# The output projection of a hybrid layer's mixed branches: eight block products, and seven by Strassen's scheme

## The chip, the cores and the metric

The kernel runs on one core of one Trainium2 chip, in one launch. The metric is the device time of that launch in microseconds, the median of several runs. The five engines that the profile shows are PE (TensorE, matmuls and transposes; PEld is its weight load), DVE (VectorE), ACT (ScalarE), POOL (GpSimd) and SP (SyncE, which here only issues transfers). Each engine works through its own instructions in order and waits at semaphores for the others.

## The reference

One layer over 512 tokens of width 1024, all in float32. Two mixers (an S5 state space model and NSA attention) run from the same normed input, a sigmoid gate weighs each, and their sum goes through the output projection `w_out`. A convolutional FFN, a gated embedding and a last norm follow.

```
n1 = rmsnorm(x, g_mix);  z = n1 @ w_in
y_ssm = s5_mixer(...);   y_nsa = nsa_mixer(...)
merge = sigmoid(z[:, OFF_MERGE:])                       # 2 x 1024 gates
mixed = merge[:, :1024] * (y_ssm @ w_br_ssm) + merge[:, 1024:] * (y_nsa @ w_br_nsa)
h = x + mixed @ w_out                                   # 512x1024 @ 1024x1024: the change is here
h = h + conv_ffn(rmsnorm(h, g_ffn), w_up, conv_w, conv_b, w_down)
h = h + sigmoid(rmsnorm(h, g_ple) @ w_ple_gate) * (p @ w_ple_proj)
return rmsnorm(h, g_final)
```

## The kernel before

A float32 product is made of three matmuls. Each operand is split into a high part (a rounded copy, made by ACT, line 75) and a low part (the difference of the operand and its high part, made by DVE or POOL, line 54); `split` writes both. `mm3` then issues high times high, high times low and low times high (lines 82, 83, 84), 128 rows by 512 columns each, into one PSUM bank.

A weight of 128 x 1024 values (two to eight blocks of 128 rows) takes four steps. SP loads it into a raw buffer `wr`, of which there are three in rotation; ACT writes `wh` and DVE or POOL writes `wl`, two of each in rotation; PE reads them. A raw buffer is free when its low part has been written, and `wh` and `wl` are free when PE has read them. `wraw` is the load alone, `wload` the load and the split.

The stages around the change, in the order in which PE meets them:

- The attention of 16 units (head and branch), with the matmuls of gates and of the SSM branch product put between its steps as filler (`fillers`, `gate`, `ssm_branch`). The last five gates run on PE with nothing between: 24 matmuls each (`pj`, eight k steps by three), high and low parts of the weights from ACT and POOL, and a tanh on ACT into `t2` (line 944).
- `oS`, the split of the attention's output `oT`, in four pieces on ACT and DVE.
- The NSA branch product: four weights of 256 columns, two tiles `br` of 12 matmuls each. DVE puts each tile onto `t2` (two instructions, line 63), and `t2` holds the mixed branches, transposed: eight blocks of 128 of the 1024 values by 512 tokens.
- The output projection. `t2` is split into `mTh` and `mTl`. `w_out` is loaded in eight pieces of 128 x 1024 and split into `w0h`, `w0l`, `w1h`, `w1l` (the two halves of the columns). Eight tiles `wo`, of four token blocks by two column halves, take 24 matmuls each and DVE adds half of each onto `hres`, which holds x.
- After two token blocks are done, their norm: squares with a sum on ACT (`sq`), a chain of small DVE instructions (`rv`, `ry`, `rt`), the scaled rows `xg`, transposes on PE (`nt`), and from them `n2h` (ACT) and `n2l` (DVE), from which the FFN's up projection reads (`ua`, `ub`). The FFN starts with the first 256 tokens.

The code gives the engines' work in one order, and a scheduler puts each engine's instructions in their final one; `issue_after` holds instructions back behind another. Buffers are shared through tags: a tile of the same tag waits until the earlier one has been read for the last time.

Of the kernel before, what the change touches and what calls it, by code (L numbers as in the profile page):

```python
# [44 lines left out]
def hybrid_kernel(ctx: ExitStack, tc: tile.TileContext, A, out):  # L45
# [1135 lines left out]
    sB.close()  # L1181

    pm_ = sY.enter_context(pool("mix", 1, "right"))
    mTh = pm_.tile([P, KD, T], F32R, name="mTh")
    w0h = pm_.tile([P, KD, 512], F32R, name="w0h")
    hres = slot(cp, "h16", [P, NQ, D], F32, "hres")
    oS = slot(pa, "kv", [P, 2, 4, T], F32R, "oS")
    with tc.issue_after(attended[0]), tc.issue_after(attended[1]):
        for i in range(4):
            split(oS[:, 0, i], oS[:, 1, i], oT[:, i])  # L1190
# [23 lines left out]
    w0l = [slot(py, "y8", [P, 4, 512], F32R, "w0l0"), slot(pa, "v8", [P, 4, 512], F32R, "w0l1")]

    w1h, w1l = (slot(p, t, [P, KD, 512], F32R, n) for p, t, n in ((po, "y16", "w1h"), (pa, "kv", "w1l")))
    for hf in range(2):
        for c in range(4):
            ks, k4 = slice(2 * c, 2 * c + 2), slice(2 * (c % 2), 2 * (c % 2) + 2)
            keep = (w1h[:, ks], w1l[:, ks]) if hf else (w0h[:, ks], w0l[c // 2][:, k4])  # L1220
            wload("w_out", D, 2 * c * P, hf * 512, 2, 512, (G, V)[hf], keep=keep)
# [5 lines left out]
    for qp in range(2):
        for hf, qt in ((0, 0), (0, 1), (1, 0), (1, 1)) if qp == 0 else ((0, 2), (1, 2), (0, 3), (1, 3)):
            cs = slice(hf * 512, hf * 512 + 512)
            qs_ = slice(qt * P, (qt + 1) * P)  # L1230
            ps = bank(either(), "wo")
            for k in range(KD):
                mm3(ps, mTh[:, k, qs_], mTl(k)[:, qs_], (w0h, w1h)[hf][:, k],
                    w1l[:, k] if hf else w0l[k // 4][:, k % 4], k == 0, k == KD - 1)
            stt(hres[:, qt, cs], ps, 0.5, hres[:, qt, cs], MUL, ADD)
# [537 lines left out]
```

## Time and profile before

| | |
|---|---|
| median of 3 runs | 799.89 us (799.82 to 800.62) |
| the profiled execution | 799.49 us, of which the span of the instructions is 797.8 us |
| granted TensorE clock | 0.998 |
| PE busy | 788.5 us, 99% of the span |
| the last five gates | 294.8 to 322.0 us |
| NSA branch product | 322.0 to 343.7 us |
| output projection | 344.1 to 390.1 us |

The profile shows one execution on the core. Busy time counts an instruction from its start to its end; matmuls overlap, so the step from one start to the next is what a matmul costs, not its length. A row of a timeline has the start, the length, the engine, the line, the operation, what it writes and reads, and in square brackets how long the engine had been idle before and who ended that.

### The profile page before, as it was taken

The page shows a single profiled execution, that of the slowest core. Times are in us where ns is not written, and L with a number is a line of the kernel's source. Part 1 is how long each engine was busy: PE and PEld are TensorE (multiplying, and loading weights), DVE is VectorE, ACT ScalarE, POOL GpSimd, SP SyncE. Part 2 cuts the span into 40 slices and gives each one's busy share as a digit, 9 for nine tenths or more (in the row PEclk, how much of TensorE's full clock was granted, in tenths as well). Part 3 has the DMA queues.
Part 4 walks back from the last instruction along what each step waited for, and adds up shares of the span by engine and source line. Part 5 has one row for each costly group of instructions (what it writes and reads, how often), then busy time and mean ns, then how long its engine had stood idle before and what let it go on. Part 6 is the DMA issues. An engine that isn't in the chain of part 4 may idle for free.

```text
span 797.8 us, 12065 instructions
## 1 busy us (share of the span) xinstructions
PE 788.5 (99%) x4438; PEld 665.5 (83%) x4438; DVE 514.3 (64%) x1085; ACT 404.0 (51%) x747; POOL 254.5 (32%) x293
## 2 busy tenths in 40 slices
PE   9999999999999999999999999999999999999996
PEld 8888898878888888878898888888888888888885
DVE  7987987976677731685454444454554667998753
ACT  6836554477677643434354344444344343584642
POOL 4577222127465533231032333332333200001221
PEclk9999999999999999999999999999999999999999
DMA  9973112234134113343042322223323342525111
GB/s 347 361 209 116 53 68 68 67 106 133 54 106 155 57 53 106 125 136 109 0 160 80 105 85 101 89 97 106 105 84 102 105 159 87 203 67 172 54 53 53
DMA packets 29852, 89.70 MB, mean 112 GB/s; under 512 B 3681, under 2 KB 6113, under 8 KB 29793
## 3 DMA queue, kind: packets, MB, share of 16 engines
q1 hardware_dynamic: 29216, 87.88, 33.4%
q10 hardware_dynamic: 576, 1.05, 0.4%
q8 instruction: 35, 0.57, 0.3%
q14 instruction: 25, 0.20, 0.1%
HBM read 79.48 MB, written 5.24 MB: 106 GB/s over the span
## 4 chain that ended last, share of the span: by engine, by line
PE 91%; DVE 5%; issue 1%; ACT 1%; DMA 0%; POOL 0%; POOLq 0%; ACTq 0%; DVEq 0%
PE pj L82 6%; PE pj L83 6%; PE pj L84 6%; PE ua L83 5%; PE ub L83 5%; PE ua L82 5%; PE ub L82 5%; PE ub L84 5%; PE ua L84 5%; PE p L84 3%; PE p L82 3%; PE p L83 3%; PE sps L1068 2%; PE ptp L1088 2%; PE wo L82 2%; PE wo L83 2%
## 5 line engine op out<-in xcount | busy, mean ns | idle before, releaser
L54 POOL TENSOR_TENSOR wl<-wr,wh 128x1024 fp32r<-128x1024 f32 x39 | 94.1, 2413 | 251.4 <-ACT wh L75 220.8
L75 ACT ACTIVATE wh<-wr 128x1024 fp32r<-128x1024 f32 x88 | 93.2, 1059 | 92.4 <-issue 29.5
L54 DVE TENSOR_TENSOR wl<-wr,wh 128x1024 fp32r<-128x1024 f32 x49 | 62.6, 1277 | 51.9 <-ACT wh L75 51.8
L82 PE MATMUL pj<-n1h,wh 128*128 128x512 f32 x224 | 91.0, 406 | 0.0
L83 PE MATMUL pj<-n1l,wh 128*128 128x512 f32 x224 | 87.7, 392 | 0.0
L84 PE MATMUL pj<-n1h,wl 128*128 128x512 f32 x224 | 87.5, 391 | 0.0
L63 DVE SCALAR_TENSOR_TENSOR cv<-ub,cols,cv 128x511 f32<-128x511 f32 (+1 forms) x44 | 32.9, 748 | 66.1 <-ACT cv L1360 65.4
L83 PE MATMUL ua<-n2l,wh 128*128 128x512 f32 (+1 forms) x176 | 66.9, 380 | 0.2 <-DVE n2l L63 0.2
L82 PE MATMUL ua<-n2h,wh 128*128 128x512 f32 (+1 forms) x176 | 66.9, 380 | 0.0
L84 PE MATMUL ub<-n2h,wl 128*128 128x512 f32 (+1 forms) x176 | 66.8, 379 | 0.0
L82 PE MATMUL ub<-n2h,wh 128*128 128x512 f32 (+1 forms) x176 | 66.8, 379 | 0.0
L83 PE MATMUL ub<-n2l,wh 128*128 128x512 f32 (+1 forms) x176 | 66.8, 379 | 0.0
L84 PE MATMUL ua<-n2h,wl 128*128 128x512 f32 (+1 forms) x176 | 66.8, 379 | 0.0
L84 PEld LDWEIGHTS pj<-n1h,wl 128*128 128x128 f32 x224 | 42.1, 188 | 9.0
L82 PEld LDWEIGHTS pj<-n1h,wh 128*128 128x128 f32 x224 | 42.1, 188 | 8.1 <-issue 0.4
L83 PEld LDWEIGHTS pj<-n1l,wh 128*128 128x128 f32 x224 | 42.2, 188 | 7.3 <-issue 0.2
L60 POOL TENSOR_SCALAR pr<-pr,su,gates 128x512 f32<-128x512 f32 (+2 forms) x64 | 39.3, 629 | 14.0 <-DVE su L1080 14.0
L75 ACT ACTIVATE ph<-ptp 128x128 fp32r<-128x128 f32 (+1 forms) x64 | 27.9, 435 | 25.8 <-PE ptp L1088 25.6
L54 DVE TENSOR_TENSOR pl<-ptp,ph 128x128 fp32r<-128x128 f32 (+1 forms) x64 | 31.0, 486 | 13.3 <-ACT ph L75 12.2
L83 PEld LDWEIGHTS ua<-n2l,wh 128*128 128x128 f32 x176 | 33.1, 188 | 6.5 <-DVE n2l L63 0.4
L84 PEld LDWEIGHTS ub<-n2h,wl 128*128 128x128 f32 x176 | 33.1, 188 | 6.3
L82 PEld LDWEIGHTS ua<-n2h,wh 128*128 128x128 f32 x176 | 33.1, 188 | 6.3
(484 smaller groups left out, 2016.2 us busy)
## 6 DMA issues: line engine op xcount, KB each, us to landing
wr<-in_w_up_dram SPq DMA_DIRECT2D x44, 512.0 KB, 3.4
wr<-in_w_in_dram SPq DMA_DIRECT2D x28, 512.0 KB, 3.5
b<-in_w_down_dram SPq DMA_DIRECT2D x14, 512.0 KB, 4.1
QQ<-QT SPq DMA_DIRECT2D x16, 256.0 KB, 4.8
wr<-in_w_out_dram SPq DMA_DIRECT2D x8, 512.0 KB, 3.5
wr<-in_w_down_dram SPq DMA_DIRECT2D x8, 512.0 KB, 3.9
wr<-in_w_ple_gate_dram SPq DMA_DIRECT2D x8, 512.0 KB, 3.5
xT<-in_x_t_dram SPq DMA_DIRECT2D x4, 512.0 KB, 9.8
```

Source lines behind the costliest of these rows:

```text
L54: e.tensor_tensor(o, a, b, op=op)
L60: e.tensor_scalar(o, a, s1, s2, op0=op0, op1=op1)
L63: e.scalar_tensor_tensor(o, a, s, b, op0=op0, op1=op1)
L75: S.activation(o, a, AF.Copy)
L82: PE.matmul(ps, lh, rh, start=start, stop=False)
L83: PE.matmul(ps, lh, rl, start=False, stop=False)
L84: PE.matmul(ps, ll, rh, start=False, stop=stop)
L1068: PE.matmul(o, self.QQ[:, x, qt * P:(qt + 1) * P], KK[:, :, self.g, :w] if both else KK[:, self.br, self.g, :w], start=x == 0, stop=x == 1)
L1088: PE.transpose(ps[:, (qt - kt) * P:(qt - kt + 1) * P], self.pr[qt][:, kt * P:(kt + 1) * P], ident)
```

## The change

The projection is cut into 2 x 2 blocks on both sides: tokens in two halves of 256, the 1024 inner values in two halves, the output columns in two halves. With a11, a12 (first token half) and a21, a22 the blocks of the mixed branches, and b11, b12, b21, b22 those of `w_out`, Strassen's scheme in Winograd's form needs seven block products instead of eight:

- sums of the mixed branches: s1 = a21 + a22, s2 = s1 - a11, s3 = a11 - a21, s4 = a12 - s2;
- sums of the weights: weight 5 is b12 - b11, weight 6 is b22 - (b12 - b11), weight 7 is b22 - b12, weight 4 is b21 - weight 6; weights 1, 2, 3 are b11, b21, b22;
- the products: 1 = a11 b11, 2 = a12 b21, 3 = s4 b22, 4 = a22 with weight 4, 5 = s1 with weight 5, 6 = s2 with weight 6, 7 = s3 with weight 7. Each is two tiles (`wo10`, `wo11` for product 1) of 12 matmuls.

The outputs are put together in `hres` with the help of `u`. In the new order the products run 1, 2, 5, 6, 3, 7, 4. The weight sums are made beside the last gates: `sums_of` loads the four blocks of `w_out` for one half j of their rows (two blocks of 128 rows each), makes the sums into `tq0` (j = 0) or `tqmaskb` and `tqmsc` (j = 1), and splits them with DVE. A step of it is issued at every sixth step of the filler after the attention. Weights 6 and 3 are split on POOL during the NSA branch product, b21 is loaded again for weight 4, whose sum and split are POOL's, too. Small tensors (`maskc`, `W2`, `W2d`, the compressor's hidden values) are laid into one tile `msc`, and `ys` is cut in two, so that their places can be used again.

The changed order has 24 fewer PE matmuls, 27 more DVE instructions, 14 more on ACT, 16 more on POOL and 4 more loads.

The loads on SP during the last gates and the first branch weights. `wr` is the raw buffer. Before:

```order
L188 DMA wr_3879<-in_w_in_dram 128x1024
L188 DMA wr_3911<-in_w_in_dram 128x1024
L188 DMA wr_3943<-in_w_in_dram 128x1024
L188 DMA wr_3975<-in_w_in_dram 128x1024
L188 DMA wr_4049<-in_w_br_nsa_dram 128x1024
```

And now:

```order
L188 DMA wr_3893<-in_w_out_dram 128x1024
L188 DMA wr_3895<-in_w_out_dram 128x1024
L188 DMA wr_3906<-in_w_in_dram 128x1024
L188 DMA wr_3941<-in_w_in_dram 128x1024
L188 DMA wr_3954<-in_w_out_dram 128x1024
L188 DMA wr_3978<-in_w_out_dram 128x1024
L188 DMA wr_3983<-in_w_in_dram 128x1024
L188 DMA wr_4008<-in_w_out_dram 128x1024
L188 DMA wr_4010<-in_w_out_dram 128x1024
L188 DMA wr_4021<-in_w_in_dram 128x1024
L188 DMA wr_4066<-in_w_out_dram 128x1024
L188 DMA wr_4091<-in_w_out_dram 128x1024
```

`wr_3893`, `wr_3895`, `wr_3954` and `wr_3978` are b11, b12, b22 and b21 of j = 0; `wr_3906`, `wr_3941`, `wr_3983` and `wr_4021` are the weights of the second to fifth of the last five gates; the first branch weight follows behind the last row. Eight loads now stand among the gates' loads, and a gate's load, which waited for POOL's low part three weights earlier, now waits for whichever instruction last read the raw buffer that it takes over: `wr_3941` for the low part of `wo1` on DVE, `wr_3954` for the low part from `wr_3906` on POOL, `wr_3983` for the second DVE difference that reads `wr_3954`, `wr_4021` for the low part from `wr_3983` on POOL.

ACT from the end of the attention on. `otmp` is the last step of the attention, `wh` the high part of a gate's weight, `t2` the tanh of a gate. Before:

```order
L75 ACTIVATE otmp_3843<-ops_3726 64x512
L75 ACTIVATE oS_4040<-oT_2235 128x512 x3
L75 ACTIVATE wh_3881<-wr_3879 128x1024
L944 ACTIVATE t2_3607<-pj_3853 128x512
L75 ACTIVATE oS_4040<-oT_2235 128x512
L75 ACTIVATE wh_3913<-wr_3911 128x1024
```

And now:

```order
L75 ACTIVATE otmp_3840<-ops_3723 64x512
L75 ACTIVATE oS_3858<-oT_2232 128x512 x3
L75 ACTIVATE wo1_3852<-wr_3893 128x1024
L945 ACTIVATE t2_3604<-pj_3866 128x512
L75 ACTIVATE oS_3858<-oT_2232 128x512
L75 ACTIVATE wh_3908<-wr_3906 128x1024
L75 ACTIVATE wo5h_3854<-tq0_3847 128x1024
L945 ACTIVATE t2_3604<-pj_3912 128x512
L75 ACTIVATE wh_3943<-wr_3941 128x1024
```

The high part of weight 1 stands where the second gate's high part stood, and the latter comes three instructions later; each later gate's high part has one or two output weights ahead of it.

PE from the last output tile into the FFN. `nt` are the transposes of the normed rows (`xg_4249` and `xg_4460` the first pair of token blocks, `xg_4589` the second), `ua` and `ub` the first FFN tiles. Before, all of the first pair's transposes stand among the output tiles, and the FFN runs on:

```order
L84 MATMUL wo_4506<-w1h_4213,mTl1_4202 128x512
L166 MATMUL nt_4566<-ident_69,xg_4249 128x128
L166 MATMUL nt_4575<-ident_69,xg_4249 128x128
L166 MATMUL nt_4584<-ident_69,xg_4249 128x128
L166 MATMUL nt_4593<-ident_69,xg_4249 128x128
L82 MATMUL ua_4621<-n2h_4247,wh_4611 128x256
```

Now (the rows are of the first FFN tile's first half):

```order
L84 MATMUL wo41_4562<-wo4h_4352,a22_4393 128x512
L82 MATMUL ub_4680<-n2h_4280,wh_4675 128x256
L83 MATMUL ub_4680<-n2l_4281,wh_4675 128x256
L84 MATMUL ub_4680<-n2h_4280,wl_4676 128x256
L82 MATMUL ub_4680<-n2h_4280,wh_4675 128x256
L166 MATMUL nt_4513<-ident_69,xg_4460 128x128 x4
L83 MATMUL ub_4680<-n2l_4281,wh_4675 128x256
L84 MATMUL ub_4680<-n2h_4280,wl_4676 128x256
L82 MATMUL ub_4680<-n2h_4280,wh_4675 128x256
L83 MATMUL ub_4680<-n2l_4281,wh_4675 128x256
```

Half of the first pair's transposes moved behind the last output tile, between matmuls that read what is made of them.

The diff, cut to its core:

```diff
     oT = slot(py, "y8", [P, 4, T], F32, "oT")
-    t1s.append(slot(po, "t16", [P, 4, T], F32, "t1b"))
+    t1s.append(slot(po, "t8h", [P, 4, T], F32, "t1b"))
...
+    W = {1: hi_lo(cp, "h16", "wo1"), 7: hi_lo(pm_, "w7", "wo7")}
+    W[5] = two((pa, po), ("ptc", "t8l"), "wo5")
+    W[2] = two((pa, py), ("v8", "y8"), "wo2")
+    def block(r, c, j):
+        return wraw("w_out", D, 2 * (2 * r + j) * P, c * 512, 2, 512)
+    def put(n, j, x, e=V):
+        for c, t in x if isinstance(x, list) else [(slice(0, 2), x)]:
+            c = slice(2 * j + c.start, 2 * j + c.stop)
+            split(W[n][0][:, c], W[n][1][:, c], t, e)
+    def sums_of(j):
+        b11 = block(0, 0, j)
+        b12 = block(0, 1, j)
+        put(1, j, b11)
+        yield
+        for c, t in tq(j):
+            tt(t, b12[:, c], b11[:, c], SUB)
+        put(5, j, tq(j))
+        yield
+        b22 = block(1, 1, j)
+        tt(b12, b22, b12, SUB)
+        for c, t in tq(j):
+            tt(t, b22[:, c], t, SUB)
+        put(7, j, b12)
+        yield
+        put(2, j, block(1, 0, j))
+        yield
...
     for _ in fill:
+        n += 1
+        if n == 4:
+            with tc.issue_after(attended[0]), tc.issue_after(attended[1]):
+                for i in range(4):
+                    split(oS[:, 0, i], oS[:, 1, i], oT[:, i])
+        if n % 6 == 0:
+            with tc.issue_after(attended[0]), tc.issue_after(attended[1]):
+                next(sums, None)
...
-            for dt_ in range(2 * d2 - 2, 2 * d2 + 2):
-                split(mTh[:, dt_], mTl(dt_), t2()[:, dt_])
+        split(a[:, 0, k2], a[:, 1, k2], x[:, :, H0])
+        if d2 < 2:
+            put(6, d2, tq(d2), G)
+            put(3, d2, block(1, 1, d2), G)
+        else:
+            y = t2()[:, 2 * d2 - 4:2 * d2 - 2]
+            tt(y[:, :, H1], y[:, :, H1], x[:, :, H1], ADD)
+            split(s1[:, 0, k2], s1[:, 1, k2], y[:, :, H1])
+            tt(y[:, :, H0], y[:, :, H1], y[:, :, H0], SUB)
...
+    def product(tag, a, n):
+        ps = [bank(tag, f"wo{n}{j}") for j in range(2)]
+        for j in range(2):
+            for k in range(4):
+                x = slice(j * P, (j + 1) * P)
+                mm3(ps[j], a[:, 0, k, x], a[:, 1, k, x], W[n][0][:, k], W[n][1][:, k], k == 0, k == 3)
+        return ps
...
+    m1 = product("s", a11, 1)
+    b21 = [block(1, 0, j) for j in range(2)]
...
+    m2 = product("acc", a12, 2)
...
+            tt(t, b21[j][:, c], t, SUB, G)
+        put(4, j, tq(j), G)
+    half_onto(0, D0, m1)
+    half_onto(0, D0, m2)
+    m5 = product("o", s1, 5)
+    m6 = product("t", s2, 6)
...
+    half_onto(0, D1, product("acc", s4, 3))
+    for j in range(2):
+        tt(hres[:, 2 + j, D1], hres[:, 2 + j, D1], u[:, 1, j], ADD, G)
+        tt(hres[:, 2 + j, D0], hres[:, 2 + j, D0], u[:, 0, j], ADD, G)
+    normed(0)
+    m7 = product("s", s3, 7)
+    half_onto(1, D1, m7)
+    half_onto(1, D0, m7)
+    half_onto(1, D0, product("o", a22, 4))
+    normed(1)
```

More of the change, by code (lines that the diff above doesn't have):

```diff
@@ L721, in hybrid_kernel @@
     with tc.issue_after(tab_at):
-        maskb = pa.tile([P, T], F32, name="maskb")
+        msc = slot(pa, "msc", [P, 512], F32, "msc")
+        maskb = slot(pa, "maskb", [P, T], F32, "maskb")
         G.memset(maskb, 0.0)
@@ L725, in hybrid_kernel @@
                         channel_multiplier=1)
-        maskc = pa.tile([P, NQ, NCMP], F32, name="maskc")
+        maskc = msc[:, 0:NQ * NCMP].rearrange("p (q n) -> p q n", q=NQ)
         G.memset(maskc, 0.0)
@@ L906, in compress @@
         kps = bank("s", "kps")
-        h1 = pa.tile([P, 64], F32, name=f"hid{i}")
+        h1 = msc[:, 384 + 64 * i:448 + 64 * i]
         pe = small("pe", 1, 2)
@@ L1177, in hybrid_kernel @@
     attended = [last(e) for e in (mybir.EngineType.DVE, mybir.EngineType.Activation)]
-    for _ in fill:
-        pass
[L1181 to L1190, printed above, removed]
@@ L1192, in hybrid_kernel, with tq @@
-    mTls = []
-    def mTl(dt_):
-        return mTls[dt_ // 4][:, dt_ % 4]
+    sB.close()
+    HT = T // 2
+    pm_ = sY.enter_context(pool("mix", 1, "right"))
+    tqs = [slot(pa, "v4", [P, 2, 512], F32, "tq0"), *(slot(pa, t, [P, 1, 512], F32, f"tq{t}") for t in ("maskb", "msc"))]
+    def tq(j):
+        return [(slice(0, 2), tqs[0])] if j == 0 else [(slice(i, i + 1), tqs[1 + i]) for i in range(2)]
+    a11, a12 = (pm_.tile([P, 2, 4, HT], F32R, name=n, tag=n, bufs=1) for n in ("a0", "a1"))
@@ new lines, in hi_lo, with two @@
+    def hi_lo(p, tag, name):
+        t = slot(p, tag, [P, 2, 4, 512], F32R, name)
+        return t[:, 0], t[:, 1]
+    def two(p, tags, name):
+        return tuple(slot(q, t, [P, 4, 512], F32R, f"{name}{x}") for q, t, x in zip(p, tags, "hl"))
+    W = {1: hi_lo(cp, "h16", "wo1"), 7: hi_lo(pm_, "w7", "wo7")}
[3 more added lines that the diff above has]
+        return wraw("w_out", D, 2 * (2 * r + j) * P, c * 512, 2, 512)
@@ new lines, in all_sums @@
+    def all_sums():
+        for j in range(2):
+            yield from sums_of(j)
+    sums = all_sums()
+    oS = slot(pa, "kv", [P, 2, 4, T], F32R, "oS")
+    n = 0
+    for _ in fill:
+        n += 1
[6 more added lines that the diff above has]
+                next(sums, None)
@@ L1198, in hybrid_kernel @@
+    for _ in sums:
+        pass
+    W[6], W[3] = hi_lo(pn, "nh", "wo6"), hi_lo(pn, "nl", "wo3")
+    s1 = s2 = None
+    H0, H1 = slice(0, HT), slice(HT, T)
     for d2 in range(4):
@@ L1208, in hybrid_kernel @@
             stt(mg, t1(dt_), 0.5, mg, MUL, ADD)
-        if d2 % 2:
-            mTls.append(slot(*((py, "t8"), (po, "t16"))[d2 // 2], [P, 4, T], F32R, f"mTl{d2 // 2}"))
-            for dt_ in range(2 * d2 - 2, 2 * d2 + 2):
-                split(mTh[:, dt_], mTl(dt_), t2()[:, dt_])
[L1214 to L1221, printed above, removed]
+        k2 = slice(2 * (d2 % 2), 2 * (d2 % 2) + 2)
@@ L1222, in hybrid_kernel @@
+    for k2 in (slice(0, 2), slice(2, 4)):
+        split(s2[:, 0, k2], s2[:, 1, k2], t2()[:, k2, H0])
+    t_ = t2()
+    tt(t_[:, 4:8, H0], t_[:, 4:8, H0], t_[:, 0:4, H0], SUB, G)
+    tt(t_[:, 0:4, H1], t_[:, 4:8, H1], t_[:, 0:4, H0], SUB, G)
     n2h = slot(pn, "nh", [P, KD, T], F32R, "n2h")
     n2l = slot(pn, "nl", [P, KD, T], F32R, "n2l")
-    xg = slot(pa, "ptc", [P, 2, D], F32, "xg")
-    for qt in range(NQ):
-        nc.sync.dma_start(hres[:, qt], dr("x", qt * P * D, [[D, P], [1, D]]))
@@ L1227, in hybrid_kernel @@
[L1227 to L1235, printed above, removed]
+    D0, D1 = slice(0, 512), slice(512, 1024)
@@ new lines, in product, with half_onto, again @@
+    def product(tag, a, n):
[5 more added lines that the diff above has]
+        return ps
+    def half_onto(r, cs, x):
+        for j in range(2):
+            o = hres[:, 2 * r + j, cs]
+            stt(o, x[j], 0.5, o, MUL, ADD)
+    def again(name, p, tag, src):
+        t = slot(p, tag, [P, 2, 4, HT], F32R, name)
+        split(t[:, 0], t[:, 1], src, G)
+        return t
@@ L1284, in hybrid_kernel @@
     NR = 4
-    HT = T // 2
     hid = []
```

34 lines of the change are left out of this document (29 added, 5 removed).

## The prediction

> **What bounds the kernel now.** I read the page first, then busy time by stage, then the timelines of each engine from 262 to 402 us.
>
> ```profile
> span 797.8 us, 12065 instructions
> PE 788.5 (99%) x4438; PEld 665.5 (83%) x4438; DVE 514.3 (64%) x1085; ACT 404.0 (51%) x747; POOL 254.5 (32%) x293
> ...
> 294.78:321.98 27.20, 27.20 (x121) 22.52 (x120) 5.35 (x6) 9.48 (x14) 9.59 (x4) 1.00 0.31 103
> 321.98:343.75 21.77, 21.77 (x97) 17.83 (x95) 17.52 (x16) 9.88 (x12) 8.78 (x4) 1.00 0.36 121
> 343.75:390.12 46.37, 46.20 (x213) 37.93 (x213) 27.85 (x57) 18.69 (x35) 4.52 (x6) 1.00 0.28 91
> 390.12:402.00 11.88, 11.65 (x99) 11.45 (x98) 6.68 (x18) 6.37 (x13) 0.52 (x1) 1.00 0.01 2
> ```
>
> The stage rows give length, then busy us of PE, PEld, DVE, ACT, POOL, the clock and DMA. They are the last five gates (27.2 us), the NSA branch product, the output projection, and the first FFN tiles. PE is the bound in each and its clock is 1.00, so a matmul taken away is worth its whole step, and a us in which PE waits costs a us.
>
> ```profile
> 294.10 0.39 PE L82 MATMUL pj<-n1h,wh 128*128 128x512 f32 x1
> 294.78 0.39 PE L82 MATMUL pj<-n1h,wh 128*128 128x512 f32 x1
> 299.54 0.39 PE L82 MATMUL pj<-n1h,wh 128*128 128x512 f32 x1
> 321.98 0.39 PE L82 MATMUL br<-oS,wh 128*128 128x512 f32 x1
> 343.51 0.39 PE L84 MATMUL br<-oS,wl 128*128 128x512 f32 x1
> 344.07 0.50 PE L82 MATMUL wo<-w0h,mTh 128*128 128x512 f32 x1 [0.17 <-DVE t L63]
> L82 PE MATMUL wo<-w0h,mTh x32: 387/389/496, 344.1 to 383.6; 128*128 128x512 f32 x32
> ```
>
> From 294.10 to 299.54 are 24 starts: 0.2267 us a matmul, though a single one lasts 0.39. G1 to G5, the last five gates (24 matmuls, 5.44 us each), start at 294.78, 300.22, 305.66, 311.10, 316.54; B0, the first NSA branch tile pair, starts at 321.98 as the trace has it.
>
> **What is removed.** The projection has six groups like the last row: 192 matmuls. Seven products of 2 x 4 x 3 make 168. 24 x 0.2267 = 5.4 us go. The start of the projection also waits now: 343.51 to 344.07 is 0.56 where 0.23 is a step, 0.3 us lost; the new order has other tiles there. Gain at most 5.7 us.
>
> **What is added beside the gates.** The output weights are read 12 times instead of 8, and the first 8 loads come among the gates' loads, in the same three raw buffers (the queue's rows above). Before, a gate's load goes out two gates ahead.
>
> ```profile
> 284.12 0.33 SPq L188 DMA_DIRECT2D wr<-in_w_in_dram  x1
> 292.51 0.33 SPq L188 DMA_DIRECT2D wr<-in_w_in_dram  x1
> ...
> wr<-in_w_out_dram SPq DMA_DIRECT2D x8, 512.0 KB, 3.5
> ...
> 294.35 1.66 ACT L75 ACTIVATE oS<-oT 128x512 fp32r<-128x512 f32 x3
> 295.91 1.05 ACT L75 ACTIVATE wh<-wr 128x1024 fp32r<-128x1024 f32 x1
> 296.98 0.60 ACT L944 ACTIVATE t<-pj 128x512 f32<-128x512 f32 x1
> 297.48 0.62 ACT L75 ACTIVATE oS<-oT 128x512 fp32r<-128x512 f32 x1
> ...
> 290.09 2.40 POOL L54 TENSOR_TENSOR wl<-wr,wh 128x1024 fp32r<-128x1024 f32 x1 [5.99 <-ACT wh L75]
> 297.04 2.40 POOL L54 TENSOR_TENSOR wl<-wr,wh 128x1024 fp32r<-128x1024 f32 x1 [4.55 <-ACT wh L75]
> ```
>
> A weight needs load 3.5, high part on ACT 1.06, low part on POOL 2.4: 6.96 us, more than the 5.44 of a gate. Today that is hidden by the lead. With two of three buffers held by output weights the lead is gone. What DVE pays beside POOL:
>
> ```profile
> 294.48 0.68 DVE L54 TENSOR_TENSOR oT<-ops,otmp 64x512 f32<-64x512 f32 x1 [5.41 <-ACT otmp L75]
> 295.19 1.90 DVE L54 TENSOR_TENSOR oS<-oT,oS 128x512 fp32r<-128x512 f32 x3
> 298.13 1.85 DVE L54 TENSOR_TENSOR oS<-oT,oS 128x512 fp32r<-128x512 f32 x1 [1.04 <-ACT oS L75]
> 317.66 1.22 DVE L54 TENSOR_TENSOR wl<-wr,wh 128x1024 fp32r<-128x1024 f32 x1 [17.67 <-ACT wh L75]
> 328.92 2.41 POOL L54 TENSOR_TENSOR w0l<-wr,w0h 128x1024 fp32r<-128x1024 f32 x1 [14.27 <-ACT w0h L75]
> 329.82 2.58 DVE L54 TENSOR_TENSOR wl<-wr,wh 128x1024 fp32r<-128x1024 f32 x1 [0.79 <-ACT wh L75]
> ```
>
> A DVE difference of 1024 columns takes 1.22 alone. Beside POOL's, which ends at 331.33, it ends at 332.40, 1.07 after: it waited out POOL's instruction. A 512 one (1.90 / 3 = 0.63) shows the same at 298.13, ending 0.54 after POOL's 299.44. I take that as the rule of the sum. The Trainium skill, SBUF — State Buffer, section "Who interferes with whom", says the same as an exclusive lock: of a DVE instruction with two SBUF inputs and a GpSimd one that reads SBUF, the later start fully blocks; the rows agree. Without such waits, only the sum's lower end below would be left.
>
> Now the chain, each hop from these rows, PE's need beside it (a gate needs the low part at its third matmul, 0.45 in; B0 at its fifth, 0.9 in):
> - G2. Its buffer is free when it was before for another gate (292.51), landed 296.0. ACT does three oS, then wo1 in the place of the gate's high part, t2, oS, and only then the high part: 298.1 to 299.15. DVE: tq0 295.2 to 296.4, oS x3 to 298.3, wo1's low part to 299.5. POOL starts then: 301.9. Needed 300.67: 1.25 lost.
> - G3. Its load waits for wo1's low part: 299.5, then 303.0, 304.1, POOL 306.5. Needed 307.4: nothing.
> - G4. Its load waits for tq0's second difference, whose operand b22 is loaded only when G2's raw weight is free: 301.9, landed 305.4; DVE waits for POOL's 306.5, two differences to 308.95; load 312.45; ACT 313.5; POOL 315.9. Needed 312.85: 3.05 lost.
> - G5. Load when G4's raw weight is free: 315.9 + 6.96 = 322.9. Needed 321.35: 1.5 lost.
> - B0. Load after three differences on DVE (1.23 + 0.63 + 0.63) that wait for POOL's 322.9: 325.4; + 3.5 + 1.06 + 1.23 on DVE = 331.2. Needed 328.8: 2.4 lost.
> Sum 8.2 us. If DVE and POOL never waited for each other the same hops end at 328.8 against an undelayed need of 322.9: 5.9. That is the lower end; I take 8.2.
>
> **After the gates.** POOL has 9.6 us of wo6 and wo3 low parts in a row (1024 columns four times, 2.4 each), and DVE must put a0's low part between them: three more such waits. The first halves of product 1 stand ahead of the third branch pair on PE, so they wait for a0: by the same arithmetic 2.4 us, nothing if POOL leaves gaps; I take 1.5. The same again for s1 and a1 beside POOL's three differences for weight 4: 0 to 1.0, I take 0.5. Products 6, 3, 7, 4 have their operands 3 us or more ahead, and cost only their matmuls. The new sums on DVE, ACT and POOL there lie beside 38 us of products.
>
> **The tail.** Before, the first norm pair's transposes lie under four tiles (21.8 us); now only products 7 and 4 (10.9 us) follow product 3.
>
> ```profile
> 374.90 1.57 ACT L169 ACTIVATE n2h<-nt,cols 128x256 fp32r<-128x256 f32 x4 [1.33 <-PE nt L166]
> 375.77 1.66 DVE L63 SCALAR_TENSOR_TENSOR n2l<-nt,cols,n2h 128x256 fp32r<-128x256 f32 x4 [3.02 <-ACT n2h L169]
> 380.94 1.03 PE L166 MATMUL nt<-ident,xg 128*128 128x128 f32 x8
> 389.96 0.69 DVE L63 SCALAR_TENSOR_TENSOR hres<-wo,hres 128x512 f32<-128x512 f32 x1 [4.70 <-PE wo L84]
> 390.56 0.28 PE L82 MATMUL ua<-n2h,wh 128*128 128x256 f32 x1
> 390.68 0.28 PE L83 MATMUL ua<-n2l,wh 128*128 128x256 f32 x1
> 391.51 0.22 DVE L60 TENSOR_SCALAR rv<-ss 128x1 f32<-128x1 f32 x1 [0.85 <-ACT sq L155]
> 393.04 0.49 DVE L58 TENSOR_SCALAR xg<-hres,ry 128x512 f32<-128x512 f32 x1
> 397.89 0.39 PE L83 MATMUL ua<-n2l,wh 128*128 128x256 f32 x1 [0.23 <-DVE n2l L63]
> ```
>
> From hres to xg is 3.6 us with nothing between. Product 3 ends at 0: hres to 0.9, squares, then hres of product 7 (waits to 3.0) stands inside the chain; xg at 5.5. The transposes of both halves end at 9.9, the first high and low parts at 11.1; PE comes to them at 11.7. But the second pair's low parts stand behind the hres of product 4 (done 12.6) and the last pair's high parts behind two squares: n2l is ready at 16.0 where PE, after 18 matmuls of 0.12 and nine transposes of 0.1, would want it at 14.8. 1.2 us lost; between 0 and 2.5 (a whole hres and squares, 0.69 + 1.55, more). The 0.23 of the last row stays.
>
> Nothing earlier moves: up to 294 us the order is the same on all engines; buffers only change names.
>
> **Sum.** 8.2 + 1.5 + 0.5 + 1.2 - 5.7 = +5.7 us on this execution's 799.5 us: 805.2. The median of the runs is 0.4 above it, so 805.6.
>
> **Rivals.**
> - The weights come too late, but less: 5.9 + 0 - 5.7 = +0.2 us, 800.1. For it: POOL and DVE alternate here in an order I only worked out. Against it: two rows that show the wait. 14%.
> - Faster: the weight sums hide beside the gates. For it: the raw loads of b11 and b12 go out over 10 us ahead (the queue's turn at 284.12 is b12's), DVE has 5.35 us of work in 27.2, and the DMA share is 0.31. Then only the tail is paid: 799.5 - 5.7 + 1.2 = 795.0, with the median's 0.4 795.4. Deciding point: each gate's load must go out 6.96 us before its third matmul; if the loads landed in under 2.0 instead of 3.5 us, five of them would make good 7.5. Against: 3.5 is the median of all. 8%.
> - PE's clock falls in the waits:
>
> ```profile
> 790.00:792.00 2.00, 0.84 (x8) 0.64 (x6) 0.83 (x3) 0.85 (x4) 0.30 (x1) 1.00 0.55 207
> 792.00:794.00 2.00, 0.00 (x0) 0.00 (x0) 1.19 (x5) 0.51 (x1) 0.55 (x1) 1.00 0.15 55
> 794.00:796.00 2.00, 0.00 (x0) 0.00 (x0) 0.24 (x1) 0.21 (x1) 0.00 (x0) 0.65 0.59 208
> ```
>
> PE's last work ends at 790.84; the clock is still 1.00 to 794 and 0.65 in the next two us, so it fell to half about 3.8 us after. My waits are 2.4 at most in one piece. If those at G4 and B0 joined into such ones and the clock stayed at half for as long, each costs 1.9: +3.8, 809.4. The Trainium skill, TensorE: Matmul & The Clock Gate, section "What's actually happening", halves the clock after an idle window of about 3.4 us; the rows agree, and that is why this has 10%.
> - The forecast, between +2 and +8.5 us: 68%.
>
> A difference under 0.2% (1.6 us) is not told from no change here. Faster 8%, same 14%, slower 78%. The range: below from the second case's 800.0, above to 809, the upper ends of the terms (8.2 + 2.4 + 1.0 + 2.5 - 5.7 = +8.4) and part of the clock's case.
>
> **What would show it.** PE's waits for POOL's wl at G2, G4 and G5 of 1 to 3 us, for B0's wh and wl together 2.4; B0 starting at 328 to 331 instead of 321.98; the queue's loads of w_in following b22 by 7 us at G4; wo with 168 matmuls at 0.227 us; waits of ub for n2l near the end. Wrong if B0 starts before 327, or if DVE beside POOL keeps to 1.2 us, or if the clock row shows less than 1.00.

## The result, and the profile after

| | before | after |
|---|---|---|
| median | 800.19 us (4 runs, 799.82 to 800.62) | 810.92 us (4 runs, 810.45 to 812.25) |
| the profiled execution, its span | 799.49 us, 797.8 us | 810.47 us, 808.7 us |
| granted TensorE clock in it | 0.998 | 0.998 |

The ratio is 1.0137, with a 95% interval of 1.0119 to 1.0154: 10.7 us slower, where 5.7 were forecast. The sign and the first half of the sum (gates and first branch pair) were right. The end of the projection was not.

Span and PE from the page of the changed kernel:

```profile
span 808.7 us, 12090 instructions
PE 787.3 (97%) x4414; PEld 661.0 (82%) x4414; DVE 553.2 (68%) x1112; ACT 413.7 (51%) x761; POOL 284.3 (35%) x309
```

PE fell from 99% to 97% of a span that is 10.9 us longer. It now waits, and the view of PE's waits says for whom (us in total, how often, the longest). Before, this view held none of these rows:

```profile
PE pj L84 <- POOL wl L54: 3.9, 3, 1.7
PE nt L166 <- DVE xg L58: 1.8, 1, 1.8
PE br L82 <- ACT wh L75: 1.6, 1, 1.6
PE pj L82 <- ACT wh L75: 1.1, 1, 1.1
PE wo L84 <- DVE s L54: 1.1, 1, 1.1
PE ub L83 <- DVE n2l L63: 1.0, 2, 0.6
PE wo L84 <- DVE a L54: 0.9, 1, 0.9
PE ub L82 <- ACT n2h L169: 0.7, 1, 0.7
```

Five of the eight are gates, the first branch pair, `a0` and `s1`, as forecast. The second row is not: a transpose that waits 1.8 us for the normed rows.

Busy time by stage, with the columns of the prediction's stage rows: the last five gates, the first two branch pairs, the rest of the branch and of the projection up to the first transpose, and the start of the FFN.

```profile
295.09:330.30 35.21, 28.58 (x121) 22.03 (x119) 24.43 (x23) 18.18 (x24) 9.60 (x4) 1.00 0.51 166
330.30:341.75 11.45, 11.39 (x48) 8.85 (x49) 8.05 (x7) 6.12 (x9) 9.99 (x5) 1.00 0.44 146
341.75:388.73 46.98, 44.98 (x196) 36.29 (x195) 44.65 (x46) 16.77 (x27) 31.89 (x16) 1.00 0.37 133
388.73:403.00 14.27, 10.72 (x60) 8.21 (x58) 12.12 (x34) 7.63 (x19) 1.99 (x6) 1.00 0.01 2
```

The gates take 35.2 us for the 27.2 of before. In the third row DVE is busy 44.65 of 46.98 us and POOL 31.89: DVE has become as full as PE. The clock is 1.00 in all four.

The end of it in single instructions. DVE's chain of the first norm:

```profile
382.20 0.21 DVE L60 TENSOR_SCALAR rv<-ss 128x1 f32<-128x1 f32 x1 [0.79 <-ACT sq L155]
382.64 0.60 DVE L63 SCALAR_TENSOR_TENSOR rt<-ry,rv 128x1 f32<-128x1 f32 x1
383.27 2.32 DVE L63 SCALAR_TENSOR_TENSOR rt<-rt 128x1 f32<-128x1 f32 x1
385.62 1.21 DVE L63 SCALAR_TENSOR_TENSOR ry<-rt,ry 128x1 f32<-128x1 f32 x1
387.36 0.73 DVE L63 SCALAR_TENSOR_TENSOR rt<-ry,rv 128x1 f32<-128x1 f32 x1
388.12 1.21 DVE L63 SCALAR_TENSOR_TENSOR ry<-rt,ry 128x1 f32<-128x1 f32 x1
389.37 1.45 DVE L58 TENSOR_SCALAR xg<-hres,ry 128x512 f32<-128x512 f32 x1
```

and what POOL does beside it, and PE behind it:

```profile
383.19 2.38 POOL L54 TENSOR_TENSOR a<-t,a 128x1024 fp32r<-128x1024 f32 x1
385.54 5.00 POOL L54 TENSOR_TENSOR hres<-hres,u 128x512 f32<-128x512 f32 x4
...
390.87 0.33 PE L166 MATMUL nt<-ident,xg 128*128 128x128 f32 x1 [1.76 <-DVE xg L58]
```

An instruction on 128 x 1 values, 0.16 us long in the kernel before, takes 2.32: it starts at 383.27, 0.08 us behind POOL's 2.38 us subtraction, and ends 0.02 us after it. The chain from `rv` to the end of `xg` takes 8.6 us (with one `hres` in its middle) where the same chain took 2.5. The kernel before, DVE and POOL:

```profile
364.14 0.21 DVE L60 TENSOR_SCALAR rv<-ss 128x1 f32<-128x1 f32 x1 [0.79 <-ACT sq L155]
364.58 0.70 DVE L63 SCALAR_TENSOR_TENSOR rt<-ry,rv 128x1 f32<-128x1 f32 x1
365.31 0.16 DVE L63 SCALAR_TENSOR_TENSOR rt<-rt 128x1 f32<-128x1 f32 x1
366.15 0.49 DVE L58 TENSOR_SCALAR xg<-hres,ry 128x512 f32<-128x512 f32 x1
...
362.86 2.40 POOL L54 TENSOR_TENSOR wl<-wr,wh 128x1024 fp32r<-128x1024 f32 x1 [17.18 <-DVE wl L54]
```

The block could be read there already. The first `rt` takes 0.70 us and ends at 365.28, 0.02 after POOL's low part; in the next chain, with POOL idle, the same instruction takes 0.22.

Where PE's time went, from the starts of its matmuls (a step is 0.2267 us, in the FFN's tiles half of it; what lies above is lost):

| | forecast | measured |
|---|---|---|
| matmuls and the old wait at the start | - 5.7 | - 5.4, and - 0.8 for the waits and restarts that the projection had before |
| G2, G3, G4, G5 | 1.25, 0, 3.05, 1.5 | 1.09, 0, 3.40, 1.62 |
| B0 | 2.4 | 2.24 |
| a0, s1 | 1.5, 0.5 | 1.33, 1.32 |
| tail | 1.2 | 5.5 |

G1 also starts 0.3 us later than before, in this execution. Together that is + 10.5; the last matmul is 10.9 later (801.42 for 790.57), and the rest lies in smaller restarts. These losses are counted from start to start. The view of waits counts the idle time alone and shows some 0.2 us less for each.

### The profile page after: what moved, and what is told of

Its sections match the earlier page's. It is cut to its first block, busy times and chain, and to the rows that moved or that the text cites. A ratio compares the mean times of both kernels' runs of the same rounds, so it can differ in the third digit from the quotient of the medians.

```text
span 808.7 us, 12090 instructions
## 1 busy us (share of the span) xinstructions
PE 787.3 (97%) x4414; PEld 661.0 (82%) x4414; DVE 553.2 (68%) x1112; ACT 413.7 (51%) x761; POOL 284.3 (35%) x309
## 4 chain that ended last, share of the span: by engine, by line
PE 83%; DVE 11%; ACT 2%; DMA 2%; issue 1%; POOL 0%; POOLq 0%; ACTq 0%; DVEq 0%
PE ua L83 5%; PE ua L84 5%; PE ua L82 5%; PE ub L83 5%; PE ub L84 5%; PE ub L82 5%; PE pj L82 5%; PE pj L83 5%; PE pj L84 5%; PE p L84 3%; PE p L83 3%; PE p L82 3%; PE sps L1069 2%; PE ptp L1089 2%; PE dn L84 2%; PE dn L83 2%
## 5 line engine op out<-in xcount | busy, mean ns | idle before, releaser
L54 DVE TENSOR_TENSOR pl<-ptp,ph 128x128 fp32r<-128x128 f32 (+1 forms) x64 | 31.0, 486 | 13.3 <-ACT ph L75 12.2
L83 PEld LDWEIGHTS ub<-n2l,wh 128*128 128x128 f32 x176 | 33.0, 188 | 7.9 <-DVE n2l L63 1.6
L82 PEld LDWEIGHTS ub<-n2h,wh 128*128 128x128 f32 x176 | 33.1, 188 | 7.2 <-ACT n2h L169 1.1
```

What stands on the lines that cost most here:

```text
L54: e.tensor_tensor(o, a, b, op=op)
L82: PE.matmul(ps, lh, rh, start=start, stop=False)
L83: PE.matmul(ps, lh, rl, start=False, stop=False)
```

## The experiments

Two theories of the 8.35 us at the gates stood open: the three shared raw buffers take the loads' lead away, or POOL and DVE, which wait for each other, make each low part late. And two of the tail: POOL's row blocks the norm's chain, or the 48 matmuls that are left as cover are too few. First the gain by itself, and each cause taken away by itself and together with another. Ratios are to the kernel before on the same chip, whose median there was 799.52 to 799.98, and 800.19 beside the changed kernel. Where two edited kernels are compared by their medians, a difference under 0.7 us can thus come from the chip.

### 24 matmuls fewer, nothing else

```diff
-            for k in range(KD):
+            for k in range(KD - 1):
                 mm3(ps, mTh[:, k, qs_], mTl(k)[:, qs_], (w0h, w1h)[hf][:, k],
-                    w1l[:, k] if hf else w0l[k // 4][:, k % 4], k == 0, k == KD - 1)
+                    w1l[:, k] if hf else w0l[k // 4][:, k % 4], k == 0, k == KD - 2)
```

> The kernel before, leaving out the last of the eight inner blocks in every output tile, so 24 matmuls fewer in the projection and nothing else changed (its output is not the layer's). Theory (PE is the bound there, a matmul is worth 0.2267 us): 24 x 0.2267 = 5.4 us less, 794.7, between 794 and 795.5. Rival (the projection's matmuls are hidden by the weight loads and splits, or given back as waits at the norm or the FFN's first tiles): 797 to 800.

Measured: 794.55 us for 799.52 of the kernel before on the same chip, ratio 0.9938 (0.9924 to 0.9953). 5.0 us of 5.4: the matmuls are worth what they take, and the scheme's own gain is real.

### Buffers of their own for the early loads, first try

```diff
+        ra, rb = (slot(pm_, f"a{x}", [P, 2, 2, 512], F32, f"raw{x}") for x in range(2))
-        b11 = block(0, 0, j)
-        b12 = block(0, 1, j)
+        b11 = block(0, 0, j, ra[:, 0])
+        b12 = block(0, 1, j, ra[:, 1])
...
-        b22 = block(1, 1, j)
+        b22 = block(1, 1, j, rb[:, 0])
...
-        put(2, j, block(1, 0, j))
+        put(2, j, block(1, 0, j, rb[:, 1]))
```

> The changed kernel, with the eight early output-weight loads in buffers of their own (the places of a0 and a1, which are filled only later), so that the three wr buffers serve the gates' weights alone as before the change. Theory (the shared buffers take the gates' lead away): the waits at G2, G4, G5 and B0, 8.35 us together in the trace of the changed kernel, go down to 1.5 at most (ACT still has output weights ahead of each gate's high part); B0 starts at 322 to 324, time 802.5, between 801.5 and 804. Rival (the order on ACT and the alternating DVE and POOL instructions hold the gates up, whatever buffer they read): the waits stay at 5 or more, time 808 to 811.

Measured: 808.98 us, ratio 1.0117 (1.0102 to 1.0133). The time is in the rival's range, 808 to 811. But G2 to G4 wait no more; G5 does, 2.3 and 1.5 us, and the last branch pair, 2.35. The queue and ACT, and then busy time by stretch, with the clock in the third column from the end:

```profile
311.24 1.94 SPq L188 DMA_DIRECT2D raw<-in_w_out_dram  x4
...
316.17 1.06 ACT L75 ACTIVATE wo2h<-raw 128x1024 fp32r<-128x1024 f32 x1 [9.05 <-DMA raw<-in_w_out_dram]
317.13 1.04 ACT L75 ACTIVATE wh<-wr 128x1024 fp32r<-128x1024 f32 x1
```

```profile
319.50:320.75 1.25, 0.00 (x1) 0.00 (x1) 0.99 (x1) 0.10 (x1) 1.19 (x1) 0.56 0.11 46
320.75:326.46 5.71, 5.71 (x14) 4.46 (x14) 5.71 (x8) 3.73 (x5) 0.00 (x0) 0.50 0.31 95
...
350.00:350.50 0.50, 0.50 (x4) 0.41 (x3) 0.50 (x1) 0.00 (x0) 0.22 (x1) 0.88 0.95 115
```

The buffers were laid out anew for the second half of the weights, so its four loads waited for all readers of the first half and went out in one burst. On ACT a high part of weight 2 waited 9.05 us for one of them, with the high part of G5's weight behind it, and behind that the tanh for which G5's first matmul waited (2.1 us in the view of waits). PE then had two waits close together and the clock fell to 0.50: 14 matmuls in 5.71 us, 0.41 each, 2.5 us more than at full clock. After the last branch pair's wait the clock fell once more (last row). So the run decides neither theory: what it lost came from the burst.

### The tail's work on DVE

```diff
-        put(4, j, tq(j), G)
+        put(4, j, tq(j), V)
...
-    a22 = again("a22", py, "t8", t_[:, 4:8, H1])
+    a22 = again("a22", py, "t8", t_[:, 4:8, H1], V)
...
-        tt(hres[:, 2 + j, D1], hres[:, 2 + j, D1], u[:, 1, j], ADD, G)
-        tt(hres[:, 2 + j, D0], hres[:, 2 + j, D0], u[:, 0, j], ADD, G)
+        tt(hres[:, 2 + j, D1], hres[:, 2 + j, D1], u[:, 1, j], ADD)
+        tt(hres[:, 2 + j, D0], hres[:, 2 + j, D0], u[:, 0, j], ADD)
```

> The changed kernel, with the low parts of weight 4, the low part of a22 and the four additions onto the second half of hres on DVE in place of POOL (POOL keeps only weight 4's differences and the low parts of s4 and s3 there). Theory (POOL's row of 128-partition instructions from 377 to 390 us blocks the small DVE instructions of the first norm, which take 0.7 to 2.3 us each): rt, ry and xg go back to 0.15 to 0.5 us, PE's waits from product 4 to the second FFN tile go from 6.1 to about 1.7, time 806.5 (805.5 to 808). Rival (the cover is short, 48 matmuls behind product 3 where 96 stood, and DVE has too much before the norm in either case): the waits stay within 1 us of 6.1, time 810 to 811.5.

Measured: 810.19 us, ratio 1.0135 (1.0118 to 1.0151), for the changed kernel's 1.0137 (1.0119 to 1.0154): no difference that can be told, and the rival's number. Three of its four runs show a clock of 0.993 or 0.994. In the two profiled executions, both at full clock, the tail loses 4.7 us for 5.5. DVE's rows say why it is not more:

```profile
382.02 1.89 DVE L54 TENSOR_TENSOR hres<-hres,u 128x512 f32<-128x512 f32 x3
...
388.42 0.21 DVE L60 TENSOR_SCALAR rv<-ss 128x1 f32<-128x1 f32 x1 [0.19 <-ACT sq L155]
```

The chain's instructions are short again, 2.5 us from `rv` to the end of `xg`, but DVE runs without a gap from 375.9 and comes to the chain at 388.42, where it had come at 382.20. What POOL had cost inside the chain, DVE now pays ahead of it.

### Both

The diffs of the last two together.

> Both edits together: own buffers for the eight early loads, and the tail's low parts and additions on DVE. Theory (the two losses are apart and add): 810.9 - 8.3 - 4.4 = 798.2, between 797 and 800, that is some 2 us faster than before the change. Rival (one of the two is not the cause): 802 to 808; both not: 811.

Measured: 807.74 us, ratio 1.0101 (1.0086 to 1.0116). 1.2 us below the run with the buffers alone, again with the wait at G5 (2.2 and 1.5 us) and a clock of 0.50 behind it. That lies at the upper end of the rival's range (802 to 808); of what the theory promised, the gates had not come. In the tail the move to DVE is worth something here: 2.9 us are lost for the 4.0 of the run with the buffers alone.

### No low part on POOL, shared buffers as they were

```diff
-            yield (lambda w, i=i: [gate(dst(i), w)]), lambda i=i: gate_weights(i0 + i)
+            yield (lambda w, i=i: [gate(dst(i), w)]), lambda i=i: gate_weights(i0 + i, V if i0 + i > 10 else G)
...
-            put(6, d2, tq(d2), G)
-            put(3, d2, block(1, 1, d2), G)
+            put(6, d2, tq(d2))
+            put(3, d2, block(1, 1, d2))
```

> The changed kernel with the low parts of the last five gates' weights and of weights 6 and 3 on DVE in place of POOL; the three shared raw buffers stay. Theory (each low part on POOL costs 2.4 us and makes DVE wait behind it, and the shared buffers pass the delay on): the chain worked out with 1.22 us low parts and no such waits gives 0 at G2, 1.0 at G4, 1.0 at G5 and 2.0 at B0, 4.0 in place of 8.35, and a0 and s1 fall from 2.65 to under 0.8: time 804.7 (803 to 806.5). Rival (only the buffers matter, the waits follow the loads whoever writes the low part): gate waits of 7 or more, time 809 to 811.

Measured: 806.52 us, ratio 1.0082 (1.0067 to 1.0097), at the upper end of the theory's range. G2 and G3 lose nothing, G4 1.74 and G5 1.53 (1.0 each expected), a0 and s1 nothing. B0 loses 4.1 instead of 2.0:

```profile
PE br L82 <- ACT wh L75: 3.9, 1, 3.9
```

Its load goes out at 322.96 and lands at 326.37, but its high part begins only at 328.20: it stands on ACT behind three of weight 6, ahead of which it stood in the changed kernel. So 1.8 of the 4.1 us come from an order that the edit changed by the way, and not from the load. Behind that wait eight matmuls ran at half clock, another 1.9 us. So POOL's low parts are one cause, and without them the loads' late issue still costs some 5.6 us (1.74, 1.53 and 2.3) of the 8.35.

### Buffers of their own, each load on its own

```diff
+    ra, rb = (slot(pm_, f"a{x}", [P, 2, 2, 512], F32, f"raw{x}") for x in range(2))
+
     def sums_of(j):
-        b11 = block(0, 0, j)
+        b11 = block(0, 0, j, ra[:, 0])
```

(and the other three as in the first try)

> As the first experiment with own buffers, but the buffers are laid out once for both rounds of weight sums, so that each of the four loads of the second round waits for the readers of its own quarter instead of all four waiting for the last and going out in one burst. Theory (in the first trial the burst of four loads at 311.2 us and the high part that waited for it ahead of G4's on ACT made the wait of 2.3 + 1.5 us, and the clock fell to 0.50 behind it): no wait above 1.5 us before B0, clock 1.00 throughout, time 803 (801.5 to 805). Rival (POOL and DVE alternate too slowly with any buffers): 806.5 to 809.

Measured: 804.58 us, ratio 1.0057 (1.0042 to 1.0072). 6.3 us below the changed kernel, with one edit, inside the theory's range and at full clock. Left are 1.25 us inside G5 for POOL, 1.2 at B0, 1.9 at the last branch pair, 1.7 at the start of product 2 and 0.5 at s1. The burst was the flaw of the first try. Neither theory of the gates is right alone: the lead is most of the loss, and what is left in G5 waits for POOL.

### All three edits

The diffs of the last two together with that of the tail's work on DVE.

> Own raw buffers with a quarter for each load, no low part on POOL from the last gates to the FFN, the additions of the second half on DVE. Theory (buffers and waits of DVE behind POOL are all of the gates' loss, POOL's block of the norm chain most of the tail's): gate waits under 1 us, a0 and s1 under 0.8, tail 2.6 as in the run with both earlier edits; against the 799.5 of before: - 5.0 (what the run with 24 matmuls fewer gained) + 1 + 0.8 + 2.3 = 798.6, between 796.5 and 800. Rival (DVE, now with all the work, becomes late itself): 801 to 806.

Measured: 797.60 us for 799.98, ratio 0.9970 (0.9961 to 0.9980): 13.3 us below the changed kernel and 2.4 below the kernel before. The stage row of this kernel's gates, and PE's waits in it, without the three (`warm`, `glu`, `ua`) that last as long in the kernel before:

```profile
294.36:321.56 27.20, 27.20 (x121) 22.53 (x120) 25.03 (x27) 17.61 (x24) 0.00 (x0) 1.00 0.65 231
```

```profile
PE ub L83 <- DVE n2l L63: 1.0, 2, 0.6
PE wo L82 <- DVE t L63: 0.3, 1, 0.3
```

27.20 us for the five gates, the number of before, with 25.03 us of DVE and none of POOL beside them, at a DMA share of 0.65. So the 11.0 us of gates, B0, a0 and s1 go when both causes are taken away. Short bandwidth of the loads is not the cause, since these gates wait for nothing at a higher DMA share than the changed kernel's 0.51. What is lost now is 0.8 us at products 2 and 5 and 2.8 at the start of the FFN.

### POOL beside the norm, in the kernel before

```diff
+        if qp == 0:
+            for _ in range(8):
+                tt(maskb, hres[:, 0, 512:], maskb, ADD, G)
         for j in range(2):
             norm(xg[:, j], hres[:, 2 * qp + j])
```

> The kernel before, with eight additions of 128x512 on POOL added, which read hres of the first token block and go out from about 363 us on, beside the first pair's norm chain (they add into a mask no longer used). Theory (an instruction of DVE with two SBUF inputs waits out the running one of POOL, however small it is): the 128x1 instructions rt and ry take up to 1.2 us each instead of 0.16, the chain from rv to xg 6 to 9 us instead of 2.5, PE waits little or not, since 96 matmuls (21.8 us) cover the chain: time 799.5 to 801. Rival (small instructions pass): they keep 0.16 to 0.25 us, time 799.5.

Measured: 804.21 us (802.03 to 805.01 in five runs), ratio 1.0046 (1.0030 to 1.0062). POOL and DVE of the slowest, the profiled one:

```profile
367.16 10.90 POOL L54 TENSOR_TENSOR maskb<-hres,maskb 128x512 f32<-128x512 f32 x8
...
366.44 0.78 DVE L63 SCALAR_TENSOR_TENSOR rt<-ry,rv 128x1 f32<-128x1 f32 x1
367.25 1.21 DVE L63 SCALAR_TENSOR_TENSOR rt<-rt 128x1 f32<-128x1 f32 x1
...
368.70 1.14 DVE L63 SCALAR_TENSOR_TENSOR rt<-ry,rv 128x1 f32<-128x1 f32 x1
370.07 1.41 DVE L58 TENSOR_SCALAR xg<-hres,ry 128x512 f32<-128x512 f32 x1
```

The chain takes 5.5 us, the second one 5.4, for 2.5 and 2.0: a little less than the 6 to 9 expected. The block is shown, in a kernel that has nothing of the change: a 128 x 1 instruction waits for POOL's 128 x 512. That the cover of 96 matmuls would hide it was wrong: the scheduler had put the first pair's transposes between the tiles, and one waits 2.5 us for the second `xg`; the clock falls, to 0.50 from 378.1 to 381.5.

### The adds held back behind the chain

```diff
     normed(0)
+    with tc.issue_after(chain[1]):
+        for j in range(2):
+            tt(hres[:, 2 + j, D1], hres[:, 2 + j, D1], u[:, 1, j], ADD)
+            tt(hres[:, 2 + j, D0], hres[:, 2 + j, D0], u[:, 0, j], ADD)
```

(on the kernel with all three edits, in the place of the four adds ahead of `normed(0)`; `chain[1]` is the last DVE instruction of the chain)

> The kernel with all three edits, with the four additions onto the second half of hres held back until the first norm's chain is issued (in the trace of that kernel they stand ahead of the chain, and DVE runs without a gap from 362 to 375 us). Theory (what is left of the tail, 2.4 us of waits of ub, comes from DVE reaching the chain late): the chain starts 1.5 to 2.5 us earlier, the waits of ub fall to 1.0 or less, time 796.1 (795.3 to 797.0). Rival (the cover of 48 matmuls is too short for transposes, high and low parts in whatever order): waits stay above 2, time 797.2 to 798.

Measured: 797.10 us, ratio 0.9968 (0.9956 to 0.9980), against 0.9970 (0.9961 to 0.9980) without it: no difference that can be told. The chain starts 2.5 us earlier (373.00 for 375.47), the first FFN matmuls do not wait, but those behind them do, 0.9 and 0.8 us at 385.6 and 386.6, for the last transposes' high and low parts, which stand behind the second pair's squares. Counted as in the table, the tail loses 2.9 us as against 2.8. The time lies between the two ranges; the waits moved some two microseconds on, as the rival has it. That no order would help is not shown.

### Half the cover, without POOL, in the kernel before

```diff
-        for hf, qt in ((0, 0), (0, 1), (1, 0), (1, 1)) if qp == 0 else ((0, 2), (1, 2), (0, 3), (1, 3)):
+        for hf, qt in ((0, 2), (0, 0), (0, 1), (1, 2), (1, 0), (1, 1)) if qp == 0 else ((0, 3), (1, 3)):
```

> The kernel before with its eight output tiles in another order: two tiles of the second pair of token blocks come ahead, so that 48 matmuls follow the first pair's last tile in place of 96, with no work on POOL beside the norm. Theory (half the cover costs by itself what the best runs still lose at the start of the FFN): the FFN's first matmuls wait 1.5 to 3 us for n2h and n2l, time 801.5 to 803. Rival (10.9 us are enough for norm, transposes and split when POOL is quiet): waits under 0.8, time 799.5 to 800.5.

Measured: 802.35 us, ratio 1.0029 (1.0018 to 1.0041). The time is the theory's, its reason is not: the start of the FFN loses one wait of 0.7 us. In the profiled execution, 3.3 us longer than that of the kernel before, 0.6 us are lost before 82 us, far ahead of the edit, and 1.9 us at 757, 360 us behind it, where both kernels issue the same instructions. DVE and POOL of this kernel there:

```profile
756.61 2.60 DVE L58 TENSOR_SCALAR xn<-hres,ry 128x512 f32<-128x512 f32 x1
...
756.56 2.37 POOL L54 TENSOR_TENSOR wg1l<-wr,wg1h 128x1024 fp32r<-128x1024 f32 x1 [5.85 <-ACT wg1h L75]
```

and of the kernel before:

```profile
754.88 0.48 DVE L58 TENSOR_SCALAR xn<-hres,ry 128x512 f32<-128x512 f32 x1
...
755.11 2.51 POOL L54 TENSOR_TENSOR wg1l<-wr,wg1h 128x1024 fp32r<-128x1024 f32 x1 [5.75 <-ACT wg1h L75]
```

Before, `xn` is 0.23 us ahead of POOL and takes 0.48. Here it is 0.05 us behind and takes 2.60. In these two executions a shift of 0.3 us settles which of the two comes first, and that costs 2 us. The Trainium skill, SBUF — State Buffer, section "Who interferes with whom", states this too: whoever issues first holds the shared ports for its whole instruction. Both traces agree.

### The tail's work back on POOL, gates in order

The kernel with all three edits, without the diff of the tail's work on DVE:

```diff
-        put(4, j, tq(j), V)
+        put(4, j, tq(j), G)
```

and `G` again for a22 and the four adds.

> The kernel with all three edits, less the one on the tail: weight 4's and a22's low parts and the four additions onto the second half of hres are POOL's again, as in the changed kernel; gates and weight sums stay without waits. Theory (POOL's row blocks the first norm's chain; the tail lost 6.1 us with it and 2.4 without): 3.4 us more than 797.6, 801.0 (800 to 802). Rival (what POOL gives up, DVE pays in front of the same chain, so that the exchange is worth the 0.7 us that it brought to the changed kernel when made alone): 798.3 (797.5 to 799.2).

Measured: 798.40 us, ratio 0.9980 (0.9971 to 0.9990): 0.8 us above the kernel with all three edits, the rival's number, with intervals that overlap a little (0.9961 to 0.9980 there). The chain is long again:

```profile
373.67 1.21 DVE L63 SCALAR_TENSOR_TENSOR rt<-rt 128x1 f32<-128x1 f32 x1
374.91 1.21 DVE L63 SCALAR_TENSOR_TENSOR ry<-rt,ry 128x1 f32<-128x1 f32 x1
...
370.76 2.86 POOL L54 TENSOR_TENSOR a<-t,a 128x1024 fp32r<-128x1024 f32 x1
```

It takes 6.4 us from `rv` to `xg`, and PE loses 4.0 us in the tail, where the changed kernel lost 5.5 and the one with the work on DVE 2.8. The last row is the low part of a22: it is over before the chain's second `rt`, which here waits out an addition of 1.28 and not, as in the changed kernel, 2.38 us.

## Why the prediction was wrong, and where it was right

- **PE bounds the stage, a matmul is worth 0.2267 us.** Right: 5.0 of 5.4 us came when the matmuls alone were left out.
- **The gates.** Right, in size and place: 8.35 us for 8.2, with no place off by more than 0.35. B0 starts at 330.30, inside the 328 to 331 that were named. The queue did what was said: b22 goes out at 301.94, the load of G4's weight 6.9 us later.

```profile
301.94 4.99 SPq L188 DMA_DIRECT2D wr<-in_w_out_dram  x2
308.81 0.33 SPq L188 DMA_DIRECT2D wr<-in_w_in_dram  x1
```

The two reasons that the sum used, late loads and DVE waiting for POOL, are the two that the runs separate: - 6.3 us with the first edit (own buffers), - 4.4 with the second (no low part on POOL), and with both (the run with the tail's work back on POOL) - 12.5. That is 1.8 more than their sum; the second edit alone also lost 1.9 us to the clock and 1.8 to the order on ACT.
- **a0 and s1.** a0 as worked out (1.33 for 1.5). s1 was mis-sized: 1.32 for 0.5, above its upper end of 1.0. Both vanish with POOL's low parts; with own buffers alone a0's goes as well, and 0.5 of s1 stays.
- **The tail: the step that failed.** It read "1.2 us lost; between 0 and 2.5", and measured 5.5. It let DVE take up product 3's `hres` at once and priced the chain from `hres` to `xg` at 3.6 us "with nothing between", the durations of a DVE that is alone; with one `hres` inside it, `xg` came at 5.5 us after product 3's end (its last matmul ends at 382.99). In the trace the later `xg`, of the second token block, is done 10.9 us after that end, and the first high part of the FFN's input starts 14.0 after it, for the 11.1 at which it was to be done. Two things were put at nothing. Weight 4's low parts, a22's and the four adds, all POOL's, lie exactly beside the chain, and the rule that the same text used at the gates (DVE waits out POOL's instruction) was not applied to instructions of 128 x 1. And the new sums, said to "lie beside 38 us of products", keep DVE busy: with POOL's work on DVE and the gates in order the chain still starts only 3.6 us after product 3's end. The runs divide the 5.5 thus:
  - 1.2 is what POOL's work beside the chain costs more than the same work on DVE ahead of it (4.0 for 2.8 with the gates in order, 4.0 for 2.9 with the buffers of the first try).
  - 1.5 goes with either edit at the gates, also where gates still wait: 4.0 are lost with own buffers, without POOL's low parts, and with both. DVE and POOL are then earlier against the products: a22's low part starts 0.2 us after product 3's end in the changed kernel, and 2.0 before it with the gates in order. Which of the two engines this helps was not separated.
  - 2.8 stay with the work on DVE. They are not POOL's, and not those of the adds, since with these held back the chain starts 2.5 us earlier and 2.9 are lost. Half the cover alone cost 0.7 in the kernel before. What the rest is was not separated. By the traces both token blocks of the second half end only with the last product, so that their `hres`, squares and scaled rows stand among the first half's high and low parts. The prediction had this for the last of them, at 1.2 us; that it makes the whole is argued, not tried.
- **The clock.** In the profiled execution it stayed at 1.00, as the forecast had it. The rival's mechanism is real all the same: it fell in the profiles of four of the edited kernels, and two of the changed kernel's four runs show 0.995 (811.38 and 812.25 us), two 0.998 and 0.997 (810.47 and 810.45). It probably fell in those two, of which there is no trace, so that the waits of this kernel stand near what it takes.
- **The range.** Its upper end added the terms' upper ends. It ended at 809 because the tail's was 2.5; with 5.5 in its place the same sum gives 811. That this is the time measured is in part luck: a0 came in below its upper end and s1 above.

## What to carry to other kernels

An instruction's duration from the trace before holds only beside the same neighbours: when a change puts POOL's work beside a chain of small DVE instructions, each of them with two inputs in SBUF may cost one whole POOL instruction, so the chain is priced by POOL's durations. Moving that work to DVE helps only as far as DVE has room: here 1.2 of 5.5 us. Loads that are put into a rotation of buffers take the lead of every later load in it, and it is worth giving them a place that is free at that time, with a separate wait for each. And when two causes feed the same waits, take both away before judging either: here one edit brought 6.3 us, the other 4.4, and only both together made seven products faster than eight, by 0.2 to 0.3%, of the 0.6% that the matmuls alone are worth.
